# A two-layer hybrid trunk on one core: another order of steps in the mixers, two queues at the beginning, and high priority at the borders

## The chip, the core and the metric

The kernel runs on one core of a Trainium2 chip. TensorE (PE) multiplies, VectorE (DVE) and ScalarE (ACT) work element by element, SyncE (SP) issues most transfers, GpSimd (POOL) does next to nothing here. The metric is the device time of one execution in microseconds (us), the median of several runs.

## The reference

The input x is 256 positions of 1024 numbers. Two layers are computed, each in three stages, and each stage adds to x:

```python
for l in range(DEPTH):                       # DEPTH = 2
    h_res = h_res + 0.5 * swiglu(rmsnorm(h_res, ffn1_norm[l]), ...)     # hidden width 2816
    z = rmsnorm(h_res, mix_norm[l]) @ w_in[l]
    zq, zk, zv, zp, hq, hi, hff, hfb, hg = split(z)
    y_att = dilated_attention(zq, zk, zv, ...)          # 8 heads of 64
    y_pool = pool_mixer(zp, ...)                        # 4 groups of 64
    y_rec = hgrn2_bidirectional(hq, hi, hff, hfb, hg, ...)   # 4 heads of 64
    h_res = h_res + concatenate([y_att, y_pool, y_rec]) @ w_out[l]
    h_res = h_res + 0.5 * swiglu(rmsnorm(h_res, ffn2_norm[l]), ...)
```

## The kernel before

All weights come in one array `w_all` of halves of 128 x 1024 numbers, in the order of use. SP loads each half into one of four `stage` buffers. Every product is made in three matmuls of f32 parts: ACT makes the high part `whi` of a half (L149), DVE the low part `wlo` (L150), and PE multiplies high by high, low by high and high by low (L168 to L170, for gates and input projection L161 to L163 too). The pool of split halves holds LOOK + 1 = 5, so the split of a later half starts only when PE is through with the half five before it. x is treated in the same way: PE turns it into `xps` (L294), ACT makes `xh` with the norm's gain (L272), DVE makes `xl` (L273). A feed-forward stage makes gates `gu`, turns the hidden values (`hp`, L352), splits them (`hi`, `lo`, L257 and L258) and multiplies them down into four accumulators `ya`, which DVE adds to x (L371).

PE works in the order in which the program is written, SP also. ACT and DVE are ordered by the framework's scheduler, which takes the program's order, priorities and explicit "issue after" marks into account. PSUM has two pools of four banks: `g` for gates, projections, scores and turns of x, `y` for accumulators, for the recurrence's levels and for the turns `tp` of P.

A mixer stage runs a string of steps from the table ORDER, one string per layer. Between the steps c:0 to c:19, which multiply one weight half of the input projection each, stand the steps of the three head groups:

- ga, gb, uv, up:m, mm:m, put:m, join are the gates and the levels of the recurrence (DVE works on `U`, `W`, `A`, `Ad`); rec, rn1 and rn2 its result (`ops`), the squares' sum (`hss`) and the norm (`rrs`). The gate `hg` is scaled and passed through ACT (`hgt`, L636 and L638) and DVE (L633, L637, L639).
- ns, nq:j and nk:j scale q and k, turn them and split them (`zq`, `zk`, `Hq`, `Lq`, `Hk`, `Lk`). sc:j makes the scores of two heads in two banks (`sc`, L692) and the softmax: DVE reads each bank in two parts with the bias into `P` and the row limit into `st` (L701), ACT takes the exponential (L704), DVE scales (L706, L708). tr:h turns P of one head into `tp` (L715), ACT copies it to `PT` (L717). pv:j multiplies with v for two heads; the results of pv:0 and pv:1 together, and of pv:2 and pv:3, are split into `hi` and `lo`.
- band makes the window sums (`pbs`, L741), pool the pooled result (`pps`, L751, split into `yh` and `yl`).
- o:pool, o:rec, o:a0 and o:a1 multiply one block of 256 rows of w_out each (24 matmuls `wo`), accumulating in the four `y` banks. a0 is heads 0 to 3, a1 heads 4 to 7. The blocks' order in `w_all` is OUT_NAMES.

At the program's start ACT's queue loads `cst` (the identity) and `prm` (gains and other parameters), SP's loads two pieces of x, the first weight half in two parts, two more pieces of x and then the weights. PE runs 12 idle matmuls (L817, 24 records in the trace) until x is there. ACT takes the squares of x (L281) for the norm.

Of the kernel before, what the change touches and what calls it, by code (L numbers as in the profile page):

```python
# [11 lines left out]
AF = mybir.ActivationFunctionType  # L12
ALU = mybir.AluOpType
# [21 lines left out]
C_PW = 78  # L35
# [5 lines left out]

HALF = 1024
IN_NAMES = ("hq", "q", "k", "zh", "hg", "v")
OUT_NAMES = ("pool", "rec", "a0", "a1")
WIDE = ("q", "k", "zh", "v")
IN_STEPS = [(nm, c) for nm in IN_NAMES for c in range(4 if nm in WIDE else 2)]

ORDER = (
    (
# [4 lines left out]
    ),  # L54
    (
# [4 lines left out]
    ),  # L60
)
LOOK = 4
FIRST = 400
# [7 lines left out]
class Trunk:  # L71
    def __init__(self, ctx, tc, x_in, wall, prm_in, rel_in, cst_in, cst2_in, msk_in, band_in, y_out):
        self.tc, self.nc = tc, tc.nc
        self.wall, self.y_out = wall, y_out
        nc = self.nc
        pool = lambda name, bufs=1, **k: ctx.enter_context(tc.tile_pool(name=name, bufs=bufs, **k))
        self.cp = pool("const")
        self.stg = pool("stage", 4)
        self.whl = pool("whl", LOOK + 1)
        self.xp = pool("xp")  # L80
        self.wk = pool("wk", 2)
        self.mx = pool("mx")
        self.pg = pool("pg", 4, space=PSUM)
        self.py = pool("py", 4, space=PSUM)
        self.dr = pool("dr", space=DRAM)

        self.stage_t, self.split_t = {}, {}
        self.n_dma = 0
        self.n_split = 0
        self.cur = 0  # L90
        self.pending = self.then = None
        self.look = LOOK

        self.x = self.cp.tile([P, 2, D], F32, name="x")
        self.prm = self.cp.tile([P, N_PRM], F32, name="prm")
        self.cst = self.cp.tile([P, N_CST], F32, name="cst")
        self.msk = self.cp.tile([P, 2 * len(LEVELS), 64], U8, name="msk")
        self.ones = self.cp.tile([P, P], F32, name="ones")
        self.bias = self.cp.tile([P, 2, 8, T], F32, name="bias")
        self.lbc = self.cp.tile([P, 3, 4], F32, name="lbc")  # L100
        self.band = self.cp.tile([P, 4, 2, T], F32, name="band")
        self.qgs = self.cp.tile([P, 8], F32, name="qgs")

        xr = x_in.rearrange("p (t d) -> p t d", t=2)
        self.ident = self.cst[:, K_ID:K_ID + P]
        nc.scalar.dma_start(self.ident, cst_in[:, K_ID:K_ID + P])
        nc.scalar.dma_start(self.prm[:, 0:C_PW], prm_in[:, 0:C_PW])
        w0 = self.stage_t[0] = self.stg.tile([P, HALF], F32, tag="stage", name="stage")
        self.n_dma = 1
        for dh in range(2):  # L110
            s = slice(dh * 512, dh * 512 + 512)
            for tt in range(2):
                nc.sync.dma_start(self.x[:, tt, s], xr[:, tt, s])
            if dh == 0:
                for j in range(2):
                    q = slice(j * HALF // 2, (j + 1) * HALF // 2)
                    nc.sync.dma_start(w0[:, q], wall[0][:, q])
        self.feed_dma(2)
        self.prm_in, self.cst_in = prm_in, cst_in
        self.bones = self.cp.tile([P, P], F32R, name="bones")  # L120
        cols = self.cp.tile([P, 4], F32, name="cols")
        self.eps, self.one = (cols[:, n:n + 1] for n in range(2))
        nc.vector.memset(self.eps, EPS)
        nc.vector.memset(self.one, 1.0)
        nc.vector.memset(self.ones, 1.0)
        self.rel_in, self.cst2_in, self.msk_in, self.band_in = rel_in, cst2_in, msk_in, band_in
# [141 lines left out]
    def parts(self, stage, k, src):  # L268

        nc = self.nc  # L270
        g = self.prm[:, C_GAIN + stage * 8 + k:C_GAIN + stage * 8 + k + 1]
        nc.scalar.activation(self.xh[:, k, :], src, AF.Copy, scale=g)  # L272
        nc.vector.scalar_tensor_tensor(self.xl[:, k, :], src, g, self.xh[:, k, :].bitcast(F32),  # L273
                                       op0=ALU.mult, op1=ALU.subtract)

# [11 lines left out]
    def turn(self, stage, dh, tt):  # L287

        nc = self.nc
        for j in range(4):  # L290
            k = 4 * dh + j
            if tt == 0 and j % 2 == 0:
                self.xps[k // 2] = self.pg.tile([P, 2, T], F32, tag="g", name="xps")
            nc.tensor.transpose(self.xps[k // 2][:, j % 2, tt * P:tt * P + P], self.x[:, tt, k * P:k * P + P], self.ident)  # L294
        if tt == 1:
            for k in range(4 * dh, 4 * dh + 4):
                self.parts(stage, k, self.xps[k // 2][:, k % 2, :])

    def rms(self, rows=False):

# [67 lines left out]

    def add(self, y, by, dh, tt, post):
        s = self.x[:, tt, dh * 512:dh * 512 + 512]  # L370
        self.nc.vector.scalar_tensor_tensor(s, y, by, s, op0=ALU.mult, op1=ALU.add)  # L371
        post(dh, tt)

    def to_stage(self, stage):
# [77 lines left out]
    def mixer(self, l):  # L452
# [335 lines left out]
        def out(nm):  # L788
            n = OUT_NAMES.index(nm)
            if n == 0:  # L790
                ys.extend(py.tile([P, 512], F32, tag="y", name="wo") for _ in range(4))
            src = V["yatt", int(nm[1])] if nm[0] == "a" else V["y" + nm]
            last = n == len(OUT_NAMES) - 1
            if last:
# [16 lines left out]
    def body(self):  # L811
        nc = self.nc
        self.new_xt()

        idle = self.pg.tile([P, 512], F32, tag="g", name="idle")
        for _ in range(12):
            self.nc.tensor.matmul(idle[:, 0:P], lhsT=self.ones, rhs=self.ones, start=True, stop=True)  # L817
        for j in range(2):
            self.split_part(0, j * HALF // 2, (j + 1) * HALF // 2)
# [7 lines left out]
                self.turn(0, 1, tt)  # L827

        def sums():
            for dh in range(2):  # L830
                for tt in range(2):
                    self.squares(0, dh, tt)

        self.pending, self.then, self.look = second, sums, 0
        for l in range(DEPTH):
# [42 lines left out]
def _out_order():  # L878
    a = np.arange
    rows = dict(a0=a(0, 256), a1=a(256, 512), pool=a(512, 768), rec=a(768, 1024))  # L880
    return np.concatenate([rows[n] for n in OUT_NAMES])

# [87 lines left out]
```

## Time and profile before

| what | value |
|---|---|
| median of 3 runs | 1022.24 us (1022.08 to 1022.24) |
| the profiled execution's own time | 1022.51 us |
| its span | 1020.7 us |
| PE busy | 1002.3 us, 98% |
| DVE busy | 606.7 us, 59% |
| ACT busy | 538.7 us, 53% |
| mean granted TensorE clock | 1.000 |

The span goes from the first to the last instruction of the profiled execution. An engine's busy time is an average over stages of different kinds: the four feed-forward stages and the two mixers (about 210 to 310 us and 720 to 815 us) load DVE quite differently. PE's idle time is what is left of the span, and the trace says for each stretch of it what ended last.

### The profile page before, as it was taken

The page shows a single profiled execution, that of the slowest core. Times are in us where ns is not written, and L with a number is a line of the kernel's source. Part 1 is how long each engine was busy: PE and PEld are TensorE (multiplying, and loading weights), DVE is VectorE, ACT ScalarE, POOL GpSimd, SP SyncE. Part 2 cuts the span into 40 slices and gives each one's busy share as a digit, 9 for nine tenths or more (in the row PEclk, how much of TensorE's full clock was granted, in tenths as well). Part 3 has the DMA queues.
Part 4 walks back from the last instruction along what each step waited for, and adds up shares of the span by engine and source line. Part 5 has one row for each costly group of instructions (what it writes and reads, how often), then busy time and mean ns, then how long its engine had stood idle before and what let it go on. Part 6 is the DMA issues. An engine that isn't in the chain of part 4 may idle for free.

```text
span 1020.7 us, 14464 instructions
## 1 busy us (share of the span) xinstructions
PE 1002.3 (98%) x5722; PEld 828.2 (81%) x5722; DVE 606.7 (59%) x811; ACT 538.7 (53%) x774; POOL 3.3 (0%) x8
## 2 busy tenths in 40 slices
PE   8999999999999999999999999999999999999998
PEld 7888788897877888888878888888877778888886
DVE  5555555689955655555565454556998465545453
ACT  7444444675765544444474444446857554444441
POOL 0000100000000000000000000000000000000000
PEclk9999999999999999999999999999999999999999
DMA  7675876544334556555655656554542345556551
GB/s 257 223 258 187 278 257 187 181 148 151 103 107 155 173 186 194 185 194 185 186 165 186 186 188 185 192 188 135 192 142 88 121 155 190 186 188 187 186 187 60
DMA packets 50276, 181.16 MB, mean 177 GB/s; under 512 B 5752, under 2 KB 6008, under 8 KB 49952
## 3 DMA queue, kind: packets, MB, share of 16 engines
q1 hardware_dynamic: 48528, 174.09, 53.4%
q0 software_dynamic: 720, 4.21, 1.2%
q10 hardware_dynamic: 960, 1.94, 0.5%
q8 instruction: 45, 0.74, 0.3%
q14 instruction: 23, 0.19, 0.1%
HBM read 179.15 MB, written 3.16 MB: 179 GB/s over the span
## 4 chain that ended last, share of the span: by engine, by line
PE 84%; DVE 8%; ACT 4%; issue 2%; DMA 1%; SPq 0%; DVEq 0%
PE gu L168 16%; PE gu L170 15%; PE gu L169 15%; PE ya L170 8%; PE ya L168 8%; PE ya L169 8%; DVE wlo L150 2%; ACT whi L149 2%; PE hp L352 2%; PE wo L168 1%; PE wo L170 1%; PE wo L169 1%; DVE P L701 1%; PE xps L294 1%; PE pv L727 1%
## 5 line engine op out<-in xcount | busy, mean ns | idle before, releaser
L150 DVE TENSOR_TENSOR wlo<-stage,whi 128x1024 fp32r<-128x1024 f32 (+1 forms) x329 | 401.4, 1222 | 350.1 <-ACT whi L149 349.3
L149 ACT ACTIVATE whi<-stage 128x1024 fp32r<-128x1024 f32 (+1 forms) x329 | 347.1, 1056 | 369.2 <-PE gu L170 200.1
L168 PE MATMUL gu<-whi,xh 128*128 128x512 f32 x704 | 275.4, 391 | 3.7 <-DVE xl L273 2.2
L170 PE MATMUL gu<-whi,xl 128*128 128x512 f32 x704 | 274.2, 390 | 0.0
L169 PE MATMUL gu<-wlo,xh 128*128 128x512 f32 x704 | 274.0, 389 | 0.0
L168 PEld LDWEIGHTS gu<-whi,xh 128*128 128x128 f32 x704 | 132.2, 188 | 33.1 <-DVE xl L273 2.9
L170 PEld LDWEIGHTS gu<-whi,xl 128*128 128x128 f32 x704 | 132.1, 188 | 28.3 <-DVE xl L273 0.9
L169 PEld LDWEIGHTS gu<-wlo,xh 128*128 128x128 f32 x704 | 132.2, 188 | 27.0
L168 PE MATMUL ya<-whi,hi 128*128 128x512 f32 x352 | 141.5, 402 | 0.0
L170 PE MATMUL ya<-whi,lo 128*128 128x512 f32 x352 | 137.7, 391 | 0.0
L169 PE MATMUL ya<-wlo,hi 128*128 128x512 f32 x352 | 137.3, 390 | 0.0
L170 PEld LDWEIGHTS ya<-whi,lo 128*128 128x128 f32 x352 | 66.0, 188 | 14.4
L169 PEld LDWEIGHTS ya<-wlo,hi 128*128 128x128 f32 x352 | 66.3, 188 | 12.6
L168 PEld LDWEIGHTS ya<-whi,hi 128*128 128x128 f32 x352 | 66.2, 188 | 12.3
L345 ACT ACTIVATE g<-gu,rc 128x256 f32<-128x256 f32 x88 | 41.4, 475 | 47.4 <-PE gu L170 47.4
L346 DVE SCALAR_TENSOR_TENSOR h<-gu,rc,g 128x256 f32<-128x256 f32 x88 | 42.0, 481 | 23.9 <-ACT g L345 23.9
L258 DVE TENSOR_TENSOR lo<-hp,hi 128x512 fp32r<-128x512 f32 x44 | 30.1, 684 | 2.8 <-ACT hi L257 2.8
L257 ACT ACTIVATE hi<-hp 128x512 fp32r<-128x512 f32 x44 | 25.5, 580 | 2.7 <-PE hp L352 2.7
L352 PEld LDWEIGHTS hp<-cst,h 128*128 128x128 f32 x176 | 21.8, 139 | 5.7
L352 PE MATMUL hp<-cst,h 128*128 128x128 f32 x176 | 26.3, 271 | 0.0
L272 ACT ACTIVATE xh<-xps,prm 128x256 fp32r<-128x256 f32 x48 | 20.5, 471 | 5.8 <-DVE xl L273 3.4
L273 DVE SCALAR_TENSOR_TENSOR xl<-xps,prm,xh 128x256 fp32r<-128x256 f32 x48 | 21.3, 478 | 2.4 <-ACT xh L272 2.2
(223 smaller groups left out, 997.5 us busy)
## 6 DMA issues: line engine op xcount, KB each, us to landing
stage<-w_all SPq DMA_DIRECT2D x327, 512.0 KB, 3.5
skew<-drow POOLq DMA_DIRECT2D x1, 2048.0 KB, 10.3
bias<-skew POOLq DMA_DIRECT2D x2, 1024.0 KB, 11.6
x<-x SPq DMA_DIRECT2D x4, 256.0 KB, 5.1
band<-band ACTq DMA_DIRECT2D x1, 1024.0 KB, 7.7
y_t<-x SPq DMA_DIRECT2D x4, 256.0 KB, 2.2
stage<-w_all SPq DMA_DIRECT2D x2, 256.0 KB, 5.5
mskf<-msk ACTq DMA_DIRECT2D x1, 320.0 KB, 5.7
```

The costliest lines, as they stand in the source:

```text
L149: nc.scalar.activation(hi[:, s], st[:, s], AF.Copy)
L150: nc.vector.tensor_tensor(lo[:, s], st[:, s], hi[:, s].bitcast(F32), op=ALU.subtract)
L168: nc.tensor.matmul(out, lhsT=ah, rhs=wh, start=start, stop=False, skip_group_check=True)
L169: nc.tensor.matmul(out, lhsT=ah, rhs=wl, start=False, stop=False, skip_group_check=True)
L170: nc.tensor.matmul(out, lhsT=al, rhs=wh, start=False, stop=stop, skip_group_check=True)
L257: self.nc.scalar.activation(hi, src, AF.Copy)
L258: self.nc.vector.tensor_tensor(lo, src, hi.bitcast(F32), op=ALU.subtract)
L272: nc.scalar.activation(self.xh[:, k, :], src, AF.Copy, scale=g)
L273: nc.vector.scalar_tensor_tensor(self.xl[:, k, :], src, g, self.xh[:, k, :].bitcast(F32), op0=ALU.mult, op1=ALU.subtract)
L345: silu = nc.scalar.activation(g2[:, tt, :], gu[tt][:, 0:256], AF.Silu, scale=r)
L346: nc.vector.scalar_tensor_tensor(h[:, tt, :], gu[tt][:, 256:512], r, g2[:, tt, :], op0=ALU.mult, op1=ALU.mult)
L352: nc.tensor.transpose(hp[:, f, tt * P:tt * P + P], h[:, tt, f * P:f * P + P], self.ident)
```

## The change

Three things are changed. In the tables, the row blocks of w_out come in the order pool, a0, rec, a1, and o:a0 follows pv:0 and pv:1 directly, o:rec follows pv:2 and pv:3; in the input projection the turns of q come later, scores later, turns of P in pairs, the band and the pooled result earlier, and rec and rn1 later, with rn2 behind c:19. At the start the first weight half goes first on SP's queue, while ACT's takes `cst`, two pieces of x, `prm` and the other two pieces; there are 9 idle matmuls instead of 12, and the squares are issued after the last copy `xh`. Throughout, the splits of x and the adds to x are issued at high priority (an offset of 400 in the scheduler's order).

```diff
-OUT_NAMES = ("pool", "rec", "a0", "a1")
+OUT_NAMES = ("pool", "a0", "rec", "a1")
...
-        "c:10 c:11 mm:8 up:16 put:8 nk:0 c:12 nk:1 mm:16 up:32 put:16 sc:0 c:13 mm:32 up:64 put:32 sc:1 "
-        "c:14 mm:64 up:128 put:64 sc:2 tr:0 c:15 mm:128 put:128 join tr:1 sc:3 c:16 tr:2 band rec rn1 c:17 rn2 tr:3 tr:4 pool c:18 tr:5 tr:6 "
-        "c:19 tr:7 o:pool pv:0 pv:1 o:rec pv:2 pv:3 o:a0 o:a1 "
+        "c:10 c:11 mm:8 up:16 put:8 c:12 nk:0 nk:1 c:13 sc:0 mm:16 up:32 put:16 c:14 sc:1 mm:32 up:64 put:32 band "
+        "c:15 sc:2 tr:0 tr:1 mm:64 up:128 put:64 c:16 sc:3 tr:2 tr:3 mm:128 put:128 join c:17 tr:4 tr:5 pool c:18 rec rn1 tr:6 "
+        "c:19 rn2 tr:7 o:pool pv:0 pv:1 o:a0 pv:2 pv:3 o:rec o:a1 "
...
-        "c:19 tr:7 o:pool pv:0 pv:1 o:rec pv:2 pv:3 o:a0 o:a1 "
+        "c:10 c:11 mm:8 up:16 put:8 c:12 nk:0 nk:1 c:13 mm:16 up:32 put:16 c:14 sc:0 mm:32 up:64 put:32 band "
+        "c:15 sc:1 mm:64 up:128 put:64 tr:0 c:16 sc:2 tr:1 tr:2 mm:128 put:128 join c:17 sc:3 tr:3 tr:4 pool c:18 rec rn1 tr:5 "
+        "c:19 rn2 tr:6 tr:7 o:pool pv:0 pv:1 o:a0 pv:2 pv:3 o:rec o:a1 "
...
-        nc.scalar.dma_start(self.prm[:, 0:C_PW], prm_in[:, 0:C_PW])
         w0 = self.stage_t[0] = self.stg.tile([P, HALF], F32, tag="stage", name="stage")
...
+        for j in range(2):
+            q = slice(j * HALF // 2, (j + 1) * HALF // 2)
+            nc.sync.dma_start(w0[:, q], wall[0][:, q])
         for dh in range(2):
             s = slice(dh * 512, dh * 512 + 512)
             for tt in range(2):
-                nc.sync.dma_start(self.x[:, tt, s], xr[:, tt, s])
+                nc.scalar.dma_start(self.x[:, tt, s], xr[:, tt, s])
             if dh == 0:
...
+                nc.scalar.dma_start(self.prm[:, 0:C_PW], prm_in[:, 0:C_PW])
...
+            with self.tc.high_priority(offset=FIRST):
+                for k in range(4 * dh, 4 * dh + 4):
+                    self.parts(stage, k, self.xps[k // 2][:, k % 2, :])
...
+        with self.tc.high_priority(offset=FIRST):
+            self.nc.vector.scalar_tensor_tensor(s, y, by, s, op0=ALU.mult, op1=ALU.add)
...
-        for _ in range(12):
+        for _ in range(9):
...
+            with self.tc.issue_after(self.copied.ins):
+                for dh in range(2):
+                    for tt in range(2):
+                        self.squares(0, dh, tt)
```

Line numbers below are those of each kernel; in the changed one most lines stand two further down. On ACT at the program's start, before, `xh` follows two parts of the first half's split, and squares stand between the copies:

```order
L106 DMA cst<-cst 128x128
L107 DMA prm<-params 128x78
L281 ACT_TABLE_LOAD
L281 ACTIVATE sq,ss<-x 128x512
L149 ACTIVATE whi<-stage 128x512 x2
L272 ACTIVATE xh<-xps,prm 128x256 x2
L281 ACTIVATE sq,ss<-x 128x512
L272 ACTIVATE xh<-xps,prm 128x256
L281 ACTIVATE sq,ss<-x 128x512
L272 ACTIVATE xh<-xps,prm 128x256
L149 ACTIVATE whi<-stage 128x1024
```

The same place in the changed kernel:

```order
L106 DMA cst<-cst 128x128
L115 DMA x<-x 128x512 x2
L117 DMA prm<-params 128x78
L115 DMA x<-x 128x512 x2
L149 ACT_TABLE_LOAD
L149 ACTIVATE whi<-stage 128x512
L272 ACTIVATE xh<-xps,prm 128x256 x2
L149 ACTIVATE whi<-stage 128x512
L149 ACTIVATE whi<-stage 128x1024
L272 ACTIVATE xh<-xps,prm 128x256 x2
```

`prm` has moved behind two pieces of x, and two splits stand between the first two copies and the next two.

On DVE in the first mixer, from the scaling of `hg` on, before (the reads L701 are those of the last score step, sc:3; ISA with `st` is the end of such a read):

```order
L633 TENSOR_TENSOR hg<-hg,r 128x512
L150 TENSOR_TENSOR wlo<-stage,whi 128x1024
L701 ISA P,st<-sc,bias 128x256
L701 ISA st 128x1
L637 SCALAR_TENSOR_TENSOR hgt<-hg,hgt 128x512
L701 ISA P,st<-sc,bias 128x256
L701 ISA st 128x1
L701 ISA P,st<-sc,bias 128x256
L701 ISA st 128x1
L639 TENSOR_TENSOR hg<-hg,hgt 128x512
```

In the changed kernel the reads there (L703) are those of sc:2, the step before the last:

```order
L635 TENSOR_TENSOR hg<-hg,r 128x512
L150 TENSOR_TENSOR wlo<-stage,whi 128x1024
L703 ISA P,st<-sc,bias 128x256
L703 ISA st 128x1
L703 ISA P,st<-sc,bias 128x256
L703 ISA st 128x1
L639 SCALAR_TENSOR_TENSOR hgt<-hg,hgt 128x512
L703 ISA P,st<-sc,bias 128x256
L703 ISA st 128x1
L525 TENSOR_TENSOR U<-U,dw 128x8x64
L525 TENSOR_TENSOR W<-W,dw 128x8x64
L641 TENSOR_TENSOR hg<-hg,hgt 128x512
```

A pair of U and W and the gate's last pass have moved in ahead of the second head's last read, which frees the bank for sc:3.

On ACT at the end of the first mixer, around the output projection, before (`hi` of `rrs` is the recurrence's split, `hi` of `pv` that of the attention):

```order
L613 ACTIVATE rrs<-hss,cols 128x512
L614 ACTIVATE rrs<-rrs 128x512
L257 ACTIVATE hi<-rrs 128x512
L717 ACTIVATE PT<-tp 128x512 x2
L756 ACTIVATE yh<-pps,prm 128x256
L149 ACTIVATE whi<-stage 128x1024
L756 ACTIVATE yh<-pps,prm 128x256
L717 ACTIVATE PT<-tp 128x512 x2
L682 ACTIVATE va<-v,rc 128x512 x2
L717 ACTIVATE PT<-tp 128x512
L149 ACTIVATE whi<-stage 128x1024 x3
L257 ACTIVATE hi<-pv 128x512
```

The same place in the changed kernel:

```order
L719 ACTIVATE PT<-tp 128x512
L684 ACTIVATE va<-v,rc 128x512 x2
L615 ACTIVATE rrs<-hss,cols 128x512
L149 ACTIVATE whi<-stage 128x1024
L616 ACTIVATE rrs<-rrs 128x512
L149 ACTIVATE whi<-stage 128x1024
L257 ACTIVATE hi<-rrs 128x512
L719 ACTIVATE PT<-tp 128x512
L149 ACTIVATE whi<-stage 128x1024
L257 ACTIVATE hi<-pv 128x512
```

The last copy `PT` has moved from ahead of the splits of the output projection's weights to behind two of them and behind `hi` of `rrs`. In the second mixer two copies stand there.

## Rows read from the trace of the kernel before

**Rows 1.** The page: busy us, share of the span and instructions of each engine; granted clock in tenths
```profile
PE 1002.3 (98%) x5722; PEld 828.2 (81%) x5722; DVE 606.7 (59%) x811; ACT 538.7 (53%) x774; POOL 3.3 (0%) x8
...
PEclk9999999999999999999999999999999999999999
```

**Rows 2.** Waits of PE: engine, line, what it waited for: us in total, times, longest
```profile
PE pbs L741 <- DVE st L701: 2.1, 2, 1.5
PE sc L692 <- DVE Lk L670: 1.6, 2, 1.2
...
PE xps L294 <- DVE x L371: 1.5, 5, 0.3
...
PE tp L666 <- DVE zq L657: 1.3, 3, 0.8
...
PE tp L666 <- DVE zk L657: 0.6, 2, 0.3
PE sc L692 <- DVE st L701: 0.5, 1, 0.5
PE pps L751 <- ACT rrs L613: 0.4, 1, 0.4
```

**Rows 3.** Windows, 260 to 270 us: stretch, length, busy us of each engine, clock, DMA share
```profile
260.00:270.00 10.00, 9.11 (x127) 7.82 (x129) 9.69 (x30) 6.32 (x18) 0.00 (x0) 1.00 0.19 57
```

**Rows 4.** Timeline, first mixer's output projection: start, us, engine, line, operation, tiles, count [idle before]
```profile
298.60 0.48 PE L168 MATMUL wo<-whi,yh 128*128 128x512 f32 x1
...
299.03 0.59 ACT L717 ACTIVATE PT<-tp 128x512 f32<-128x512 f32 x1
...
301.64 1.06 ACT L149 ACTIVATE whi<-stage 128x1024 fp32r<-128x1024 f32 x1 [1.07 <-PE wo L170]
...
303.93 0.39 PE L170 MATMUL wo<-whi,yl 128*128 128x512 f32 x1
```

**Rows 5.** Timeline, the beginning of the program, some rows of PE and ACT
```profile
1.12 5.49 PE L817 MATMUL idle<-ones 128*128 128x128 f32 x24 [1.12 <-DVE ones L125]
...
6.39 1.25 PE L294 MATMUL xps<-cst,x 128*128 128x128 f32 x8
...
8.27 0.82 ACT L272 ACTIVATE xh<-xps,prm 128x256 fp32r<-128x256 f32 x2
...
27.49 0.60 PE L352 MATMUL hp<-cst,h 128*128 128x128 f32 x4
```

**Rows 6.** DMA issues of the first 16 us: tiles, queue, count, KB each, us to landing
```profile
x<-x SPq DMA_DIRECT2D x4, 256.0 KB, 5.1
...
prm<-params ACTq DMA_DIRECT2D x1, 39.0 KB, 4.5
```

**Rows 7.** Groups by line and shape: busy us, mean ns of one, idle before
```profile
L150 DVE TENSOR_TENSOR wlo<-stage,whi 128x1024 fp32r<-128x1024 f32 x327 | 400.0, 1225 | 348.6 <-ACT whi L149 347.8
...
L701 DVE CUSTOM_DVE_ANT_0 P<-sc,bias 128x256 f32<-128x256 f32 x32 | 12.0, 418 | 0.5 <-PE sc L692 0.5
...
L258 DVE TENSOR_TENSOR lo<-pv,hi 128x512 fp32r<-128x512 f32 x4 | 2.8, 692 | 0.9 <-ACT hi L257 0.9
...
L257 ACT ACTIVATE hi<-pv 128x512 fp32r<-128x512 f32 x4 | 2.4, 599 | 3.4 <-PE pv L727 3.4
```

**Rows 8.** Timeline of DVE, first mixer, the gate `hg`
```profile
277.34 0.69 DVE L633 TENSOR_TENSOR hg<-hg,r 128x512 f32<-128x512 f32 x1
...
280.83 0.69 DVE L637 SCALAR_TENSOR_TENSOR hgt<-hg,hgt 128x512 f32<-128x512 f32 x1 [1.33 <-ACT hgt L636]
```

**Rows 9.** Timeline of PE, first mixer: a level, a head's turns, two heads' scores, the next product
```profile
275.29 0.37 PE L556 MATMUL lev<-U,W 64*128 64x128 f32 x1
...
276.38 0.66 PE L715 MATMUL tp<-cst,P 128*128 128x128 f32 x4
276.97 0.39 PE L692 MATMUL sc<-Hk,Hq 64*128 64x256 f32 x2
...
277.86 0.50 PE L168 MATMUL v<-whi,xh 128*128 128x512 f32 x1
```

More of the change, by code (lines that the diff above doesn't have):

```diff
@@ L112, in __init__ @@
             for tt in range(2):
-                nc.sync.dma_start(self.x[:, tt, s], xr[:, tt, s])
+                nc.scalar.dma_start(self.x[:, tt, s], xr[:, tt, s])
             if dh == 0:
-                for j in range(2):
-                    q = slice(j * HALF // 2, (j + 1) * HALF // 2)
-                    nc.sync.dma_start(w0[:, q], wall[0][:, q])
+                nc.scalar.dma_start(self.prm[:, 0:C_PW], prm_in[:, 0:C_PW])
         self.feed_dma(2)
@@ L271, in parts @@
         g = self.prm[:, C_GAIN + stage * 8 + k:C_GAIN + stage * 8 + k + 1]
-        nc.scalar.activation(self.xh[:, k, :], src, AF.Copy, scale=g)
+        self.copied = nc.scalar.activation(self.xh[:, k, :], src, AF.Copy, scale=g)
         nc.vector.scalar_tensor_tensor(self.xl[:, k, :], src, g, self.xh[:, k, :].bitcast(F32),
@@ L295, in turn @@
         if tt == 1:
-            for k in range(4 * dh, 4 * dh + 4):
-                self.parts(stage, k, self.xps[k // 2][:, k % 2, :])
+            with self.tc.high_priority(offset=FIRST):
+                for k in range(4 * dh, 4 * dh + 4):
+                    self.parts(stage, k, self.xps[k // 2][:, k % 2, :])
     def rms(self, rows=False):
@@ L370, in add @@
         s = self.x[:, tt, dh * 512:dh * 512 + 512]
-        self.nc.vector.scalar_tensor_tensor(s, y, by, s, op0=ALU.mult, op1=ALU.add)
+        with self.tc.high_priority(offset=FIRST):
+            self.nc.vector.scalar_tensor_tensor(s, y, by, s, op0=ALU.mult, op1=ALU.add)
         post(dh, tt)
@@ L829, in sums @@
         def sums():
-            for dh in range(2):
-                for tt in range(2):
-                    self.squares(0, dh, tt)
+            with self.tc.issue_after(self.copied.ins):
+                for dh in range(2):
+                    for tt in range(2):
+                        self.squares(0, dh, tt)
         self.pending, self.then, self.look = second, sums, 0
```

6 rows, old and new, of the table ORDER are left out of this document.

## The prediction

> **What bounds the kernel now.** The page's busy times come first: TensorE (PE) works 1002.3 us of a span of 1020.7, so only some 18 us of the span are PE's to win, and any PE work that starts later than now is lost at once [rows 1]. The waits of PE say what those microseconds are. Inside the two mixers PE waits for the band (`pbs`) 2.1 us, for scores (`sc`) 1.6 and 0.5, for turns of q and k (`tp` from `zq`, `zk`) 1.3 and 0.6, for `pps` 0.4: 6.5 us together [rows 2]. At the five borders between stages it waits for the added x and for the split of x; the row of `xps` has its five of them [rows 2]. The reader should see there that nearly every releaser is VectorE (DVE), though DVE is busy only 59% of the span [rows 1]. The mixers tell why: in 260 to 270 us DVE works 9.69 of 10 us [rows 3]. There DVE has no slack, and a step that is asked for later is ready later only as long as DVE has room for it.
>
> The kernel has a second queue of this sort. ScalarE (ACT) makes the high half `whi` of every weight half in 1.06 us, and it may do so only when PE has finished an older half, since the pool of halves has five buffers. Whatever stands in ACT's order behind such a split waits with it. In the output projection the split at 301.64 us starts 3.04 us after the first `wo` product at 298.60, right after PE's twelfth product [rows 4].
>
> **The beginning.** The forecast is about when the first gate turn `hp` can run, 27.49 us now, which is 19.2 after the first split of x (`xh`, 8.27) [rows 5]. Now `prm`, which `xh` needs, is the second transfer on ACT's queue; after the change it is the fourth, behind two pieces of x. That queues don't move data for each other's account is seen in the issues: the 39 KB of `prm` took 4.5 us beside pieces of x of 256 KB that took 5.1 [rows 6]. So I expect `prm` and the second piece of x up to a microsecond later than now, and `xh` at T = 8.2, between 7.8 and 9.5: the half weight split ahead of `xh` is one instead of two, which gives some of it back. The Trainium skill (page "Trainium Kernel Development and Optimization", section Key Constraints) says that transfers from SP's, ACT's and GpSimd's queues run on the same 16 DMA engines and interleave, so that a second issuing queue saves issue time alone; the transfer rows above agree. Taken at its word, the 512 KB of x would share with as much weight, an estimate of 0.8 to 1.6 us more at the 325 GB/s that those engines reach there; the sum would then start from T = 9.1 to 9.9, and the total below would grow by about 1.
>
> Behind T, in the new ACT order, the second pair of `xh` stands behind two more splits (half of 1.06, then 1.06) and ends at about T + 2.9; its `xl` on DVE stands behind the `wlo` of the same half, 1.22 [rows 7], and ends at T + 4.2. PE's sixth product needs it. From there 67 products at 0.228 are 15.3 (24 `wo` products start between 298.60 and 303.93, the first 0.09 longer than the rest [rows 4]: 5.24 over 23); eight turns add 0.9 and one wait for a later `xl` 0.25. `hp` comes at T + 20.6 = 28.8, which is 1.3 later. Moving the squares behind the last copy of x costs nothing: the scale that they give is needed by the first gate, which comes out at about the same T + 20. There is one cost more. The idle matmuls (24 records) start 5.49 / 24 = 0.23 us apart [rows 5], where four turns of that size take 0.59 with the change of work counted, 0.15 apart [rows 9]; although the page's line of the granted clock reads 9 from its first slice on [rows 1], this is the pace of the lower level, 1.2 GHz. It lasts about as long as the idle run, and work follows at once [rows 5]. With nine instead of twelve the run ends near 5.2, and PE then stands until x is there, so part of the first products may run at half pace. Most of that hides behind the wait for the sixth product's `xl`. I take 0.7, between 0 and 2. **Together +2.0, between 0 and +4.6.**
>
> **Waits removed in the input projections.** The scores, turns of q and k and the band stand behind whole column steps (2.7 us of PE) more than now, so the 6.5 us of waits go [rows 2]. Joined turns save a little: the first product after a turn takes 0.48 where others take 0.39 [rows 4], 0.1 for each of three excursions that vanish per mixer, 0.6 in all. **-7.1.** This term could be smaller, not larger.
>
> **New waits there.** DVE's order, not PE's, now decides. In the first mixer `hg` is scaled right as sc:2 begins, and `hgt` needs two passes on ACT after that: now it starts 2.8 us after the end of `hg` (277.34 + 0.69, and 280.83) [rows 8]. In the new order the second head's first read of sc:2 stands behind this `hgt`, and the second behind a pair of U and W and the next `hg`: counted from sc:2's start, `hg` ends at 0.65 and `hgt` runs at 3.45; then come 0.6 for it, 0.35 for a read (0.42, overlapped) [rows 7], 1.2 for U and W, which are as large as `hgt`, 0.6 for `hg` and 0.5 for reciprocal and read: 6.7. PE has its twelve score products (276.97 to 277.86, 0.9), eight turns (four take 276.38 to 276.97; 1.0 together), a level (275.29 to 276.38, 1.1) [rows 9] and twelve products, 2.7: together 5.7. Then it wants the bank for sc:3: a wait of 1.0. In the second mixer the same chain meets sc:2; U and W run there before `hgt`, while ACT is still at it, so 0.7 is left. The `pps` product there waits for the first head's reads of sc:3, which DVE does behind a `wlo` whose `whi` can't start before PE's last product of c:17: 1.06 + 1.15 + 0.7 = 2.9, against 0.9 and 1.0 on PE, leaves 1.1. Waits of 0.4 (the low part of k before sc:0, first mixer) and 0.2 (W before a level, second), read off in the same way, come on top. **+3.4, between 0 and +7**: nothing if DVE is ahead of this by two microseconds, twice that if it falls behind earlier.
>
> **The output projection.** Here two things change which the trace prices well. First, o:a0 now follows pv:0 and pv:1 directly. PE used to have o:rec's 24 products meanwhile; now it waits for `hi` from `pv` (0.60) and for `lo` (0.69) [rows 7], less the two products that need `hi` alone: 1.0 in each mixer. Secondly, the last turns of P (tr:7, and tr:6 in the second mixer) hold accumulator banks that `wo` takes over. Their copies `PT` stood ahead of the gated split (299.03 now [rows 4]) and now stand behind it and behind `hi` of `rrs`, because rn2 is issued after c:19. So they are done at 3.04 + 1.0 + 0.5 + 0.6 = 5.2 us after `wo`'s first product [rows 4, 7]. Product 19, which takes the fourth bank, would start at 4.1: a wait of 1.1 in the first mixer. In the second the third bank is held too, and product 13 would start at 2.8: a wait of 2.4. **+5.5, between +2 and +7.** Moving the row block of a0 ahead of rec costs nothing by itself, the bytes are the same.
>
> **The borders.** High priority for the adds and the splits moves no instruction at the five borders: ACT's and DVE's orders are the same there, so the waits in the row of `xps` stay [rows 2]. 0.
>
> **The sum** on the profiled execution, 1022.51: 2.0 - 7.1 + 3.4 + 5.5 = +3.8, 1026.3. The median of the runs is 0.27 lower: about 1026.0.
>
> **Rivals.** (1) DVE keeps pace and the beginning costs 1: the new input-projection waits are nothing, and what is won there is paid back in the output projections, 1.0 - 7.1 + 5.5 = -0.6, about 1021.6, no change. For it: PE's new waits rest on sums of DVE rows with a margin of 1 us. Against it: DVE at 9.69 of 10 in just that stretch [rows 3]. (2) Faster: as (1), and the copies `PT` aren't late, because ACT's gated split turns out to be early (another half leaves the pool sooner): -7.1 + 2.0 + 1.0 = -4.1, about 1018. Against it stands that the row of that split names PE's `wo` product as its releaser [rows 4]. (3) Worse: DVE falls behind from the first score on and the beginning runs long at the low level: 4.6 - 7.1 + 7 + 5.5 = +10, about 1032. (4) That a part doesn't do what it says is in the forecast already, the high priority. If it did act, the five waits of `xps` would be shorter by at most 1.5 us [rows 2], which changes no sign.
>
> **The numbers.** The forecast, slower, has 0.57; rival 1 has 0.18, rival 2 0.13, rival 3 0.12. What a measurement of this kernel tells from no change is 0.2%, 2 us. Faster by more than that: rival 2 and a little of rival 1, 0.15. Within it: most of rival 1 and the low edge of the forecast, 0.20. Slower: the rest, 0.65. The range goes from 1019.5, which takes in rival 1, to 1032, at the terms' upper ends.
>
> **What would show it.** In the profile after: `hp` first at 28 to 30 us; no wait of PE for `zq`, `zk` and the band; waits of `sc` and `pps` for DVE's `st`, 3 to 4 us in all; waits of `wo` for `PT` at about 1.1 and 2.4 and for `hi` and `lo` of `pv` at about 1 each. The forecast is wrong if PE has no wait at `wo`, or if the waits of `sc` there stay under 1 us together.

## The result and the profile after

The changed kernel takes 1028.76 us (median of six runs, 1027.39 to 1030.99) where the kernel before takes 1022.03 beside it. The ratio is 1.0069, with a 95% interval of 1.0057 to 1.0081. It is slower, as forecast; the forecast was 1026.0 in a range of 1019.5 to 1032.0. Before, six runs lie within 0.5 us of each other; after, they spread over 3.6 us. The spread goes with TensorE's mean granted clock, which is 0.993 in the two longest runs and 0.997 in the two shortest, though one run between them shows 1.000 (the last section comes back to this). The profiled execution is one of the longest of the six: 1030.99 us with a span of 1029.2, 8.5 more than the span before. Where times of stretches are compared below, they are those of this execution.

The page of the changed kernel, busy times and the granted clock in 40 slices:

```profile
PE 1007.3 (98%) x5716; PEld 830.3 (81%) x5716; DVE 606.3 (59%) x811; ACT 538.8 (52%) x774; POOL 3.3 (0%) x8
...
PEclk8999999999999999999999999999999999999999
```

Against [rows 1], DVE and ACT do the same work in the same time, and PE is busy 5.0 us longer, although three idle matmuls (six records, 1.3 us) are gone and the rest of its instructions are the same. So more than half of the loss is not in waits: it is in instructions that last longer. The first digit of the clock line is now 8.

The waits of PE in the changed kernel (what it waited for: us in total, times, longest):

```profile
PE wo L168 <- ACT PT L719: 3.3, 2, 2.2
PE xps L294 <- DMA x<-x: 2.9, 2, 1.8
...
PE pps L753 <- DVE st L703: 1.5, 1, 1.5
...
PE xps L294 <- DVE x L373: 1.5, 5, 0.3
PE wo L168 <- ACT hi L257: 1.4, 2, 0.7
PE sc L694 <- DVE st L703: 1.3, 2, 0.7
...
PE lev L546 <- DVE W L525: 0.2, 1, 0.2
```

Beside [rows 2]: the waits for the band, for `Lk` and for the turns of q and k are gone, all 6.5 us with those that stood at `sc` and `pps` for other reasons. New are `PT` at `wo` (1.1 and 2.2), `hi` at `wo` (0.7 twice), `pps` (1.5), scores (0.7 and 0.5), a level (0.2). The five border waits for x are exactly as before, 1.5 in 5. And there is a wait for x itself at the beginning, 2.9, which was not there at all.

The stretches of the two mixers, each from the first `ga` to a landmark behind it (the next stage's first `gu`, and `hp` of the last stage), in the kernel before (stretch, length, busy us of PE, PEld, DVE, ACT, POOL, granted clock, DMA share, GB/s):

```profile
199.90:327.50 127.60, 123.20 (x1145) 102.62 (x1145) 96.51 (x181) 83.69 (x150) 0.00 (x0) 1.00 0.41 133
703.90:847.90 144.00, 139.74 (x1221) 116.27 (x1222) 105.97 (x186) 94.95 (x166) 0.00 (x0) 1.00 0.43 134
```

and between the same landmarks in the changed one:

```profile
204.80:331.70 126.90, 123.28 (x1144) 102.23 (x1144) 95.77 (x181) 84.11 (x150) 0.00 (x0) 1.00 0.41 134
708.20:856.40 148.20, 142.03 (x1221) 117.37 (x1222) 106.33 (x186) 94.70 (x166) 0.00 (x0) 0.99 0.42 131
```

The first mixer begins 4.9 us later and is 0.7 shorter; the second is 4.2 longer; what lies between and behind differs by 0.1. In the second, PE's busy time grew by 2.3, and the granted clock is 0.99.

### The profile page after: what moved, and what is told of

The parts are those of the page before. It is cut to its first block, busy times and chain, and to the rows that moved or that the text cites. A ratio compares the mean times of both kernels' runs of the same rounds, so it can differ in the third digit from the quotient of the medians.

```text
span 1029.2 us, 14456 instructions
## 1 busy us (share of the span) xinstructions
PE 1007.3 (98%) x5716; PEld 830.3 (81%) x5716; DVE 606.3 (59%) x811; ACT 538.8 (52%) x774; POOL 3.3 (0%) x8
## 4 chain that ended last, share of the span: by engine, by line
PE 91%; DVE 4%; ACT 3%; DMA 1%; issue 1%; ACTq 0%; DVEq 0%
PE gu L168 16%; PE gu L170 16%; PE gu L169 16%; PE ya L170 8%; PE ya L168 8%; PE ya L169 8%; PE hp L353 2%; PE wo L168 1%; PE wo L170 1%; PE lev L546 1%; PE wo L169 1%; ACT whi L149 1%; DVE wlo L150 1%; PE xps L294 1%; PE zh L168 1%; PE pv L729 1%
## 6 DMA issues: line engine op xcount, KB each, us to landing
bias<-skew POOLq DMA_DIRECT2D x2, 1024.0 KB, 10.2
band<-band ACTq DMA_DIRECT2D x1, 1024.0 KB, 8.3
```

## The beginning: the second queue

The first rows of the changed kernel's beginning, in order of time (start, us, engine, line, operation):

```profile
1.12 4.21 PE L819 MATMUL idle<-ones 128*128 128x128 f32 x18 [1.12 <-DVE ones L125]
7.12 0.63 PE L294 MATMUL xps<-cst,x 128*128 128x128 f32 x4 [1.79 <-DMA x<-x]
8.89 1.11 PE L294 MATMUL xps<-cst,x 128*128 128x128 f32 x4 [1.14 <-DMA x<-x]
...
10.73 0.63 PE L169 MATMUL gu<-wlo,xh 128*128 128x512 f32 x1
...
18.96 0.40 PE L169 MATMUL gu<-wlo,xh 128*128 128x512 f32 x1
...
32.35 0.60 PE L353 MATMUL hp<-cst,h 128*128 128x128 f32 x4
```

The second piece of x is there at 8.89, where both pieces were there by 6.39 before [rows 5]. `xh` starts at 9.61 instead of 8.27, and `hp` at 32.35 instead of 27.49. From 10 to 18 us a product takes 0.63 where it later takes 0.40. The granted clock of two stretches shows why:

```profile
9.00:11.00 2.00, 1.86 (x6) 1.36 (x7) 1.92 (x7) 1.39 (x4) 0.00 (x0) 0.50 0.95 383
13.00:20.00 7.00, 6.93 (x23) 5.32 (x22) 5.42 (x8) 4.29 (x6) 0.00 (x0) 0.58 0.90 270
```

0.50 is the lower level, 1.2 GHz. PE had stood for 1.79 us just before, ahead of the first turns of x, and for 1.14 ahead of the second.

Five runs take the beginning apart. In the first, only the transfers are put back:

```diff
+        nc.scalar.dma_start(self.prm[:, 0:C_PW], prm_in[:, 0:C_PW])
...
-        for j in range(2):
-            q = slice(j * HALF // 2, (j + 1) * HALF // 2)
-            nc.sync.dma_start(w0[:, q], wall[0][:, q])
...
-                nc.scalar.dma_start(self.x[:, tt, s], xr[:, tt, s])
+                nc.sync.dma_start(self.x[:, tt, s], xr[:, tt, s])
...
-                nc.scalar.dma_start(self.prm[:, 0:C_PW], prm_in[:, 0:C_PW])
+                for j in range(2):
+                    q = slice(j * HALF // 2, (j + 1) * HALF // 2)
+                    nc.sync.dma_start(w0[:, q], wall[0][:, q])
```

> The changed kernel with the transfers at the beginning as before (x first on SP's queue, prm second on ACT's); 9 idle matmuls, late squares and high priority stay. Theory: the queues are the cause of nearly the whole loss at the beginning. x is there at 6.4, PE's idle stretch ahead of it is 1 us instead of 1.8 and 1.1, xh starts at 8.3, and hp comes at 27.5 to 28.5: 4 to 4.8 less than the changed kernel, 1024 to 1024.7. Rival: nine idle matmuls or the order with squares last cost as much by themselves: hp at 30 or later, 1026.5 or more.

It took 1024.06 us (1.0026, 1.0015 to 1.0038), 4.7 less than the changed kernel. Its beginning:

```profile
4.75 0.64 PE L294 MATMUL xps<-cst,x 128*128 128x128 f32 x4
5.58 0.66 PE L294 MATMUL xps<-cst,x 128*128 128x128 f32 x4 [0.19 <-DMA x<-x]
...
26.56 0.60 PE L353 MATMUL hp<-cst,h 128*128 128x128 f32 x4
```

`hp` comes at 26.56, which is 5.8 earlier than in the changed kernel and 0.9 earlier than before the change. Executions of one beginning differ, so the other traces have to be read beside these: `hp` comes at 30.50 to 31.75 in three more with the changed beginning, at 26.92 and 26.93 in two more with the one before, and at 25.93 and 26.31 in two more with this one. On the means the transfers cost 5.1 us, and the other three parts of the new beginning (nine idle matmuls, late squares, high priority), which no run takes apart, give 0.8 back. x is ready for the turns from 4.75 on, since the shorter idle run no longer stands in front of them.

Is it `prm`, as the prediction has it, or x? The second run only puts `prm` ahead of x on ACT's queue:

```diff
+        nc.scalar.dma_start(self.prm[:, 0:C_PW], prm_in[:, 0:C_PW])
...
-            if dh == 0:
-                nc.scalar.dma_start(self.prm[:, 0:C_PW], prm_in[:, 0:C_PW])
```

> The changed kernel with prm second on ACT's queue, ahead of x, as before; x stays on ACT's queue, the weights stay first on SP's. The step of the prediction: it is prm, behind two pieces of x, that is late; then xh comes at about 8.3 and hp at 29 or earlier, 1025.5. Rival: x itself is late, since its pieces share the transfer engines with as many bytes of weights, prm only arrives with them; then the second piece of x is there at 9 us as in the changed kernel, hp is at 31 to 32.5 and the time 1028 to 1029.

1028.34 us, no better than the changed kernel. `prm` took 3.6 us, and x was as late as ever:

```profile
8.99 1.94 PE L293 MATMUL xps<-cst,x 128*128 128x128 f32 x8 [3.67 <-DMA x<-x]
```

The third run keeps the weights first, but issues x on the same queue behind them (`prm` second on ACT's queue):

```diff
-                nc.scalar.dma_start(self.x[:, tt, s], xr[:, tt, s])
+                nc.sync.dma_start(self.x[:, tt, s], xr[:, tt, s])
```

> The changed kernel with everything but cst and prm on SP's queue, the first weight half in two parts first, then x: one queue, the weights ahead. If what delays x is the number of bytes that are moved ahead of it or with it, one queue or two is all the same: the second piece of x arrives at about 9 us, hp is at 31 to 32.5, 1028 to 1029. If the second queue itself is bad, x is there earlier than in the changed kernel, hp before 30, 1026 or less.

Of the two outcomes the second came. Both pieces of x were there at 5.74, `hp` came at 26.14, and the kernel took 1024.82 us. It differs from the run before it in the queue of x alone, and is 3.5 us shorter. The issues of the first 16 us of this run (count, KB each, us from issue to landing):

```profile
x<-x SPq DMA_DIRECT2D x4, 256.0 KB, 4.6
```

and of the changed kernel:

```profile
x<-x ACTq DMA_DIRECT2D x4, 256.0 KB, 7.6
...
prm<-params ACTq DMA_DIRECT2D x1, 39.0 KB, 6.9
```

So it is not the weight half ahead of x that hurts. On one queue the weights of the *next* halves stand behind x; with x on its own queue SP goes on to issue them (its second half at 1.65 us, against 3.92), and they take part of the transfer engines, which are full (DMA share 0.93 to 1.05 from 3 to 9 us). The rows of the two queues (packets, MB, share of the 16 engines; q1 is SP's, q10 ACT's) show how much had been moved when the second piece of x was there. On one queue, up to 5.74 us:

```profile
q1 hardware_dynamic: 625, 1.15, 60.3%
q10 hardware_dynamic: 288, 0.11, 6.9%
```

On two, in the changed kernel, up to 9 us:

```profile
q1 hardware_dynamic: 505, 1.35, 42.9%
q10 hardware_dynamic: 787, 1.03, 35.3%
```

One queue had moved 1.26 MB, little more than what was needed: `cst`, `prm`, the first weight half and two pieces of x are 1.15 MB together. Two queues had moved nearly twice as much. 1.35 MB of it were weights, and ACT's queue itself had moved 1.03 MB where `cst`, `prm` and the two pieces are 0.63, so parts of the third and fourth piece went ahead as well. The Trainium skill (page "DMA: Bandwidth & Descriptors", section "Queues, rings and completion order") says that each transfer engine goes round the queues that have work for it; the landing times above agree, 7.6 us against 4.6. Here a queue of its own was worth a share, and a place ahead on the common queue was worth a priority. Whether ACT's queue is the slower one by itself is not tested: no run has x there without weights beside it.

The fourth and fifth run try to save the clock alone, with 14 idle matmuls instead of 9, and with 12 and three more between the pairs of turns.

```diff
-        for _ in range(9):
+        for _ in range(14):
```

> The changed kernel with 14 idle matmuls instead of 9; ACT's and DVE's orders stay. The idle run then ends at about 7.6 us instead of 5.3. Theory: of the 4.8 us at the beginning, PE's fall to the lower granted clock (0.5 from about 8.7 to 18.9 us) costs 2 and the later x and prm the rest. With PE busy until x is there the clock stays at 1.0, xh is still at 9.6, and hp comes at about 30.3: 2 us less than the changed kernel, about 1026.7. Rival: the splits behind xh set hp whatever PE's pace, hp stays at 32.3 and the time at 1028.7. A third way: the second piece of x, at 8.9 us, makes PE idle again and the clock falls all the same.

```diff
-        for _ in range(9):
-            self.nc.tensor.matmul(idle[:, 0:P], lhsT=self.ones, rhs=self.ones, start=True, stop=True)
+        def warm(n):
+            for _ in range(n):
+                self.nc.tensor.matmul(idle[:, 0:P], lhsT=self.ones, rhs=self.ones, start=True, stop=True)
+
+        warm(12)
...
-        for tt in range(2):
+        for tt, n in ((0, 3), (1, 0)):
             self.turn(0, 0, tt)
+            warm(n)
```

> The changed kernel with 12 idle matmuls ahead of the first turns of x, as before the change, and 3 more between the two pairs of turns, where PE waited for the second piece of x. Theory: PE has then no long idle stretch before the first product, works at full pace from there (0.40 us a product instead of 0.63), and hp comes at about 30 instead of 32.3: 1026.5. Rival: it is the gap behind the third product, where PE waits for the second pair of xh, that drops the clock (as with 14 idle matmuls, whose first products took 0.50 and whose fourth took 0.80): hp at 31.5, 1028 to 1029.

1029.91 and 1029.62 us: nothing won. For the second run this is its rival. For the first it is nearly its third way, but the fall comes one wait later than was said there. In the run with 14, PE's first product came quicker, and the fourth, behind a wait of 0.96 us for `xh`, is slow again:

```profile
9.64 0.50 PE L168 MATMUL gu<-whi,xh 128*128 128x512 f32 x1 [0.35 <-ACT xh L272]
...
11.83 0.80 PE L168 MATMUL gu<-whi,xh 128*128 128x512 f32 x1 [0.96 <-ACT xh L272]
...
31.49 0.60 PE L353 MATMUL hp<-cst,h 128*128 128x128 f32 x4
```

As long as x is late, PE stands in several places, and filling one of them leaves the next. `hp` at 31.49 instead of 32.35 is within what executions differ by: in the run with the turns early (below), whose beginning is the changed kernel's own, it came at 30.96. How much of the 4.9 us is the late x and how much the clock can be separated only roughly. The first product comes 1.4 later (10.14 against 8.78). From there to `hp` it is 22.2 us against 18.7 before. In the run with `prm` first, whose products are back at 0.40 from 13.66 on, it is 20.2. So an estimate from these traces is 1.4 for the later first product, 2 for the slow products and turns behind 13.66, and 1.5 for what lies ahead, the first slow products and the splits of x that come late.

## The mixers

First the tables alone: the kernel before with OUT_NAMES and ORDER of the change and nothing else.

```diff
-OUT_NAMES = ("pool", "rec", "a0", "a1")
+OUT_NAMES = ("pool", "a0", "rec", "a1")
...
-        "c:19 tr:7 o:pool pv:0 pv:1 o:rec pv:2 pv:3 o:a0 o:a1 "
+        "c:19 rn2 tr:7 o:pool pv:0 pv:1 o:a0 pv:2 pv:3 o:rec o:a1 "
```

> The tables of the change (ORDER and OUT_NAMES) with the beginning and the priorities of before. Theory: the loss has two parts that add up. The beginning costs 4.8 us (first hp at 32.3 us against 27.5 in the traces), the mixers 3.5 (first -0.7, second +4.2). So this kernel has hp at 27.5 again and takes 1022.0 + 3.5 = 1025.5, its mixers waiting as in the changed kernel: wo for PT 1.1 and 2.2, pps 1.5, with a lower granted clock behind the wait of 2.2. Rival: the mixers' tables are neutral or better by themselves and suffer only from a beginning that runs late: 1022 or less.

And the rest alone: the changed kernel with both tables as before.

```diff
-OUT_NAMES = ("pool", "a0", "rec", "a1")
+OUT_NAMES = ("pool", "rec", "a0", "a1")
...
-        "c:19 rn2 tr:7 o:pool pv:0 pv:1 o:a0 pv:2 pv:3 o:rec o:a1 "
+        "c:19 tr:7 o:pool pv:0 pv:1 o:rec pv:2 pv:3 o:a0 o:a1 "
```

> The beginning and the priorities of the change with the tables of before. Theory: hp at about 32.3 us, everything behind it as before, 1022.0 + 4.8 = 1026.8, perhaps 2 us less in runs where the clock falls for a shorter time. The borders keep their waits (xps for x 1.5 us in 5), since high priority moves nothing there. Rival: high priority shortens the five borders, each by some tenths, and the sum is 1025 or less with hp at 32.3.

The tables alone take 1024.82 us, 2.7 more than before (1.0027, 1.0015 to 1.0038); the beginning alone 1026.38, 4.2 more (1.0041, 1.0026 to 1.0056). Together they make 6.9, and the whole change made 6.7: the two parts add up. The beginning alone has before's five waits for x at the borders to the tenth, 1.5, so the high priority did nothing there.

The tables' six runs fall in two groups: 1023.8 to 1024.0 where the granted clock over the span is 1.000, and 1025.6 to 1025.8 where it is 0.997 or 0.998. The profiled execution of the changed kernel shows the place (that of the tables alone, one of the longer group, shows the same), the second mixer's output projection. ACT and PE there, in order of time:

```profile
808.50 1.06 ACT L149 ACTIVATE whi<-stage 128x1024 fp32r<-128x1024 f32 x1 [1.36 <-PE wo L170]
809.46 0.61 ACT L257 ACTIVATE hi<-rrs 128x512 fp32r<-128x512 f32 x1
809.98 1.06 ACT L719 ACTIVATE PT<-tp 128x512 f32<-128x512 f32 x2
```

```profile
808.07 0.39 PE L170 MATMUL wo<-whi,yl 128*128 128x512 f32 x1
810.61 0.63 PE L168 MATMUL wo<-whi,yh 128*128 128x512 f32 x1 [2.15 <-ACT PT L719]
...
814.37 0.40 PE L168 MATMUL wo<-whi,yh 128*128 128x512 f32 x1
...
815.15 1.95 PE L729 MATMUL pv<-PT,va 128*64 128x256 f32 x16
...
817.79 0.50 PE L168 MATMUL wo<-whi,hi 128*128 128x512 f32 x1 [0.70 <-ACT hi L257]
818.13 0.40 PE L169 MATMUL wo<-wlo,hi 128*128 128x512 f32 x1
818.52 0.50 PE L170 MATMUL wo<-whi,lo 128*128 128x512 f32 x1
```

The copy `PT` stands behind the gated split and behind `hi` of `rrs`, as the prediction has it, and PE waits 2.15 us. The nine products after that take 3.76 us from the first start to 814.37. From 810 to 815 us the granted clock is 0.66:

```profile
810.00:815.00 5.00, 4.39 (x12) 3.32 (x12) 1.42 (x2) 1.04 (x3) 0.00 (x0) 0.66 0.52 173
```

In the run with the old transfers the same wait stands in the same place, and the granted clock stays at 1.00 behind it:

```profile
802.29 0.39 PE L170 MATMUL wo<-whi,yl 128*128 128x512 f32 x1
804.83 0.50 PE L168 MATMUL wo<-whi,yh 128*128 128x512 f32 x1 [2.15 <-ACT PT L719]
...
807.79 1.95 PE L729 MATMUL pv<-PT,va 128*64 128x256 f32 x16
```

From the twelfth product to the first `pv` it is 5.50 us there and 7.08 in the changed kernel: 1.6 more, close to the 1.8 between the two groups of runs. Without the wait the same stretch takes 3.04 (800.13 to 803.17 in the first of the best kernels below). So a wait of 2.15 us cost 4.0 where the clock fell, and 2.5 where it didn't. Two runs undo the two new causes in the output projection one by one. First, the last turns go ahead of c:19, so that their copies are ahead of the gated split on ACT:

```diff
-        "c:15 sc:2 tr:0 tr:1 mm:64 up:128 put:64 c:16 sc:3 tr:2 tr:3 mm:128 put:128 join c:17 tr:4 tr:5 pool c:18 rec rn1 tr:6 "
-        "c:19 rn2 tr:7 o:pool pv:0 pv:1 o:a0 pv:2 pv:3 o:rec o:a1 "
+        "c:15 sc:2 tr:0 tr:1 mm:64 up:128 put:64 c:16 sc:3 tr:2 tr:3 mm:128 put:128 join c:17 tr:4 tr:5 pool c:18 rec rn1 tr:6 tr:7 "
+        "c:19 rn2 o:pool pv:0 pv:1 o:a0 pv:2 pv:3 o:rec o:a1 "
...
-        "c:19 rn2 tr:6 tr:7 o:pool pv:0 pv:1 o:a0 pv:2 pv:3 o:rec o:a1 "
+        "c:19 rn2 o:pool pv:0 pv:1 o:a0 pv:2 pv:3 o:rec o:a1 "
```

> The changed kernel with tr:7 (first mixer) and tr:6 tr:7 (second) ahead of c:19 instead of behind it. On ACT their copies PT then stand ahead of the splits that wo gates. Theory: the waits of wo for PT (1.1 and 2.2 us) go, and with the second the lower clock behind it (0.66 granted over 810 to 815 us, 1.7 us): 5.0 less, about 1023.7, unless the turns now wait for the softmax of sc:3, which would give back up to 1 in each mixer. Rival: the accumulators' banks are late for another reason, or the turns take the wait over in full: 1028.7.

1024.31 us, 4.45 less than the changed kernel. The wait for `PT` is gone from the list, no other wait has grown, and between the landmarks above the mixers are 1.4 and 4.1 shorter. Secondly, the output projection's blocks in their old order, all else as changed:

```diff
-OUT_NAMES = ("pool", "a0", "rec", "a1")
+OUT_NAMES = ("pool", "rec", "a0", "a1")
...
-        "c:19 rn2 tr:7 o:pool pv:0 pv:1 o:a0 pv:2 pv:3 o:rec o:a1 "
+        "c:19 rn2 tr:7 o:pool pv:0 pv:1 o:rec pv:2 pv:3 o:a0 o:a1 "
```

> The changed kernel with the order of the output projection of before: rows pool, rec, a0, a1 and o:rec between the two pairs of pv. Theory: the waits of wo for hi of pv go (0.7 twice) with the 0.15 that the low part costs behind each, 1.7 together; the waits for PT stay, with the clock's fall behind the second: 1028.7 less 1.7 is 1027.0, the state of the clock at the beginning adding up to 2 either way. Rival: the recurrence's split, which is late now, makes o:rec wait in place of o:a0 for 1 us or more, and nothing is won.

1027.77 us, 1.0 less, where 1.7 was expected. In its trace the waits for `hi` are gone and the mixers are 1.0 and 1.1 shorter, 2.1 together; the spread of the runs (1027.07 to 1028.35 here, 1027.39 to 1030.99 for the changed kernel) is larger than the difference of the medians, which is not clear of noise, so the median says less than the trace. The recurrence's split was in time.

Now the parts that help can be put together. The first version takes before's beginning, the change's input projections, the early turns and the old order of the output projection. Its difference from the kernel before is ORDER alone, whose last line is now

```diff
-        "c:19 tr:7 o:pool pv:0 pv:1 o:rec pv:2 pv:3 o:a0 o:a1 "
+        "c:19 rn2 o:pool pv:0 pv:1 o:rec pv:2 pv:3 o:a0 o:a1 "
```

> The beginning, the priorities and the output projection's order of before, the input projections of the change, and tr:7 (tr:6, tr:7) ahead of c:19. Theory: of before's 6.5 us of waits in the mixers all go, and 3.0 come (sc 1.3, pps 1.5, a level 0.2); no wait for PT, none for hi of pv: 1022.1 - 3.5 = 1018.6. Rival: DVE, which is nearly full in the mixers, sends the waits elsewhere, and the time is 1021 or more.

1018.22 us (0.9965, 0.9952 to 0.9978): faster than both, and 0.4 from the sum. The second version has the new beginning with the old transfers as well, and a third moves the second mixer's `pool` behind c:18:

```diff
-        "c:15 sc:1 mm:64 up:128 put:64 tr:0 c:16 sc:2 tr:1 tr:2 mm:128 put:128 join c:17 sc:3 tr:3 tr:4 pool c:18 rec rn1 tr:5 tr:6 tr:7 "
+        "c:15 sc:1 mm:64 up:128 put:64 tr:0 c:16 sc:2 tr:1 tr:2 mm:128 put:128 join c:17 sc:3 tr:3 tr:4 c:18 pool rec rn1 tr:5 tr:6 tr:7 "
```

> All that has helped so far in one kernel: the beginning of the changed kernel with the transfers of before (hp at 26.6 in the run with the old transfers, 27.5 before), the input projections of the change, tr:7 (tr:6, tr:7) ahead of c:19, and the output projection's order of before. Theory: the parts add up; the kernel with the beginning of before took 1018.2 and had its hp at 26.9, so this one takes 1018 or up to 0.5 less. Rival: nine idle matmuls leave the clock low in some executions, and the time is 1019 or more.

> The kernel of the run before this one, with the pooled result of the second mixer behind c:18 instead of ahead of it. Theory: pps waited 1.5 us because DVE's reads of sc:3 stand behind a wlo whose whi waits for PE's last product of c:17; with the twelve products of c:18 (2.7 us) between, the wait goes and no other comes: 1.5 less. Rival: the rec step that then stands where pps stood, or the turns tr:6 and tr:7, take the wait over: no change.

1017.45 us (0.9956, 0.9943 to 0.9968) and 1016.05 us (0.9941, 0.9928 to 0.9953). The 0.8 between the first two fits `hp`, which comes at 26.93 in the first and at 25.93 in the second, but their intervals overlap. The 1.4 of the third is the wait at `pps`. Its list of PE's waits has nothing left from inside the mixers but

```profile
PE sc L694 <- DVE st L703: 1.3, 2, 0.7
...
PE lev L546 <- DVE W L525: 0.2, 1, 0.2
```

so the input projections as the change has them were worth 3.75 us (the first version), and with the pooled result behind c:18 they are worth about 5. The beginning (4.2 by its own run) and the output projection (6.4: the 2.7 that the tables alone lost and these 3.75) took almost three times the 3.75.

## Why the prediction was right, and where its sizes were off

**What bounds the kernel**, and the two queues that decide (DVE's in the mixers, ACT's behind a gated split): right. PE's waits in the mixers are the ones named, from the releasers named.

**The beginning, +2.0 between 0 and +4.6: measured 4.9 in the trace, 4.2 in the run of the beginning alone.** This is the term that failed; `hp` came at 32.35, where 28 to 30 was the sign to look for. It failed in two steps. The first is the step "`prm` and the second piece of x up to a microsecond later". The second piece came at least 2.5 later (8.89 against 6.39, and against 5.58 in the run with the old transfers). `prm` was late too (its first reader on DVE starts at 9.0 instead of 5.7), but it was not the cause, and a start of `xh` at 8.2 became 9.61. Behind this step stands the reading of [rows 6] that queues don't move data for each other's account. The row doesn't show that: 39 KB took nearly as long as 256 KB, and in the changed kernel SP's queue took more than half of what was moved while x was waited for. The sentence on the Trainium skill's rule gave 9.1 to 9.9, and 9.61 lies within it. That one half split less stands ahead of `xh` gains nothing when x is what is waited for. The second step is the 0.7 for products at half pace: "Most of that hides behind the wait for the sixth product's `xl`." The low level lasted to the thirteenth product and the next turns of x, past that wait. From `xh` to `hp` the prediction had 20.6; it was 22.7. That the rest of the new beginning, the late squares among it, costs nothing held, as far as its three parts together tell.

**Waits removed, -7.1: measured -6.5.** All of them went. The 0.6 for joined turns was not found: the first mixer's -0.7 is the difference of its waits alone (3.4 before; 1.1 + 0.7 + 0.7 and 0.15 for `lo` after).

**New waits in the input projection, +3.4: measured 3.0.** sc:3 in the first mixer 0.7 (worked out as 1.0), sc:2 in the second 0.5 (0.7), `pps` 1.5 (1.1, though 2.9 less 0.9 and 1.0 is 1.0), the level 0.2 (0.2), the low part of k none (0.4). Together `sc` and `pps` made 2.8, a little under the 3 to 4 of the sign. The chain through `hgt` was real. In the first mixer of the changed kernel it runs

```profile
280.01 0.69 DVE L639 SCALAR_TENSOR_TENSOR hgt<-hg,hgt 128x512 f32<-128x512 f32 x1
280.62 0.42 DVE L703 CUSTOM_DVE_ANT_0 P<-sc,bias 128x256 f32<-128x256 f32 x1
...
282.17 0.68 DVE L641 TENSOR_TENSOR hg<-hg,hgt 128x512 f32<-128x512 f32 x1
...
282.85 0.40 DVE L703 CUSTOM_DVE_ANT_0 P<-sc,bias 128x256 f32<-128x256 f32 x1
...
283.32 0.38 PE L694 MATMUL sc<-Hk,Hq 64*128 64x256 f32 x1 [0.74 <-DVE st L703]
```

that is 3.3 us from `hgt` to the scores, where the prediction had 6.7 - 3.45. Rival 1, that DVE keeps pace, fell.

**The output projection, +5.5: measured 5.0 in waits and 1.6 in clock.** `PT` 1.1 and 2.2 (worked out as 1.1 and 2.4), `hi` with `lo` 0.85 each (1.0; the rows alone give 0.60 + 0.69 less two products of 0.23, 0.83). What was missing is that the clock can be lower behind a wait of this length, as it was in six of the eight traces that have it: that is a cost behind the wait, not in it, and the prediction looked for it only at the beginning. Rival 2, that the gated split comes early, fell at 808.50.

**The borders, 0:** right, 1.5 us in five waits before and after.

The terms as measured, 4.9 - 6.5 + 3.0 + 6.6, make 8.0 of the 8.5 by which the span of the profiled execution grew; the 0.5 that are left lie mostly in the second mixer and are not accounted for. Against the sum of +3.8 the median grew by 6.7. The sign came out for the reasons given, and the size was too small, by 2.9 at the beginning and 1.1 in the output projection. That the forecast is still within 3 us of the median is in part luck: the median has 1.8 less of the loss than the execution whose terms are listed here.

## What to carry to other kernels

A transfer that the first instructions need is better placed on the common queue, ahead of what can wait, than on a queue of its own, where in this kernel it shared the engines with whatever the other queue issued next. When a table of steps is moved, look for the copies that free an accumulator: put them ahead of any split that waits for the very products that need the accumulator. A wait of PE of two microseconds in a dense stretch should be priced with the slow products that can follow it.

## What was not expected of the hardware

In every trace here the granted clock reads 1.00 in the first microseconds, while PE works at the low pace. The idle records show it in the run with 14 idle matmuls (those records alone: stretch, length, busy us of PE and PEld with their counts, granted clock, DMA share, GB/s):

```profile
3.00:4.00 1.00, 1.00 (x6) 1.00 (x6) 1.00 1.00 318
4.00:5.00 1.00, 1.00 (x11) 1.00 (x10) 1.00 0.86 262
```

The same instruction comes 6 times in one microsecond and 11 times in the next, and the column does not change. In the run with the early turns products took 0.63 us up to 16 us with the column at 1.00 throughout,

```profile
9.00:11.00 2.00, 1.86 (x6) 0.96 (x4) 1.97 (x6) 1.86 (x4) 0.00 (x0) 1.00 0.98 395
...
13.00:20.00 7.00, 6.93 (x28) 5.53 (x28) 5.81 (x8) 4.90 (x9) 0.00 (x0) 1.00 0.91 314
```

so at a program's start the pace must be read from the products and not from that column. And the same wait of 2.1 to 2.2 us was followed by the lower level in some executions and not in others: in six of the eight traces that have it the granted clock falls behind it, in two (the old transfers, and `prm` first) it stays at 1.00. Three of six runs of the tables alone were 1.8 us longer than the other three. What decides between the two is not shown here.
